# The entry of an output stage: order of the branch weights, buffers of the gates, staging of the last matrix

## The chip, the cores and the metric

The kernel runs on one core of a Trainium2 chip, in one launch. The metric is the device time of one execution in microseconds (us); the lower the better.

## What is computed

One layer of a streaming encoder, for 2048 prompt frames and 64 sample frames of 1024 channels. An input projection makes the parts of two branches (differential attention and retention), a gate path for each branch and two merge gates. The end of the layer is what matters here:

```python
def layer_output(x, oa, ob, za, zb, ga, gb, subln_g, lam_init, w_oa, w_ob, w_out):
    B, T = x.shape[0], x.shape[1]
    oa = (rmsnorm(oa, subln_g) * (1.0 - lam_init)).reshape(B, T, W_A) * jax.nn.silu(za)
    ob = rmsnorm(ob).reshape(B, T, W_B) * jax.nn.silu(zb)
    m = ga * (oa @ w_oa) + gb * (ob @ w_ob)
    return x + m @ w_out
```

`ga` and `gb` have gone through a sigmoid with a bias. `w_oa` and `w_ob` are 512 x 1024 (the branch weights `w_o_diff` and `w_o_ret`), `w_out` is 1024 x 1024.

## The kernel before

Every product keeps float32 accuracy by splitting each operand in a high part (a cast to a shorter float32, on ScalarE, ACT) and a remainder (a subtraction, on VectorE, DVE, or GpSimd, POOL), and by three matmuls: high x high, high x remainder, remainder x high.

The program is written out by a planner that runs while the kernel is built. Each piece of work is a generator with a priority (the second argument of `spawn`, small first). A generator yields a time or a condition; the planner keeps a model of the clock of each engine (`P`, `A`, `V`, `G`, `ld`) and always goes on with the first generator by priority that is ready on TensorE's (PE's) modelled clock. The order in which it emits instructions is the order on PE, ACT and DVE; on POOL and on SP's queue, from which all loads and stores are issued, the scheduler below it may issue an instruction earlier, once its buffer is free. `take` and `give` count the buffers of a tag; `BUFS` holds how many a tag has. Semaphores follow from the buffers.

Two streams share PE. `w_stream` does the input projections (L384) in two halves and ends the first part of the kernel; `z_stream` does attention and retention between them. When `z_stream` ends, its buffers are freed, the pool `z3` is opened there, and `load_wo` (priority 3) and `out_prep` (priority 1) are started, while PE is still in the last projections. `load_wo` brings each of the eight 128-row tiles of the branch weights in four pieces of 256 columns through `split_load` and `split_fin` (L1232, L1235, L1239), staged in buffers of the tag "oz". `out_prep` waits until the last weight tile has been set up, and then loads, for each group of 264 frames (256 prompt and 8 sample frames) and each of 8 tiles (4 per branch), a branch output `on` and its gate `z`; `og_fin` makes `on * silu(z)` with a third buffer `sg` and splits it (L1284 to L1301). These are the gated tiles, `ogh` and `ogl`.

When `w_stream` ends, its buffers are freed too and the pool `z4` is opened. `out_stream` (priority 8) then does PE's work of the output stage; `gate_prep` (priority 0) brings the merge gates, two buffers of the tag "gt" for each tile, and `load_wout` (priority 2) brings `w_out` in 32 pieces of 256 columns, staged in the same tag "gt", six buffers in all.

For each of 8 groups, `out_stream` runs 8 m tiles (L1339 to L1341), each 24 matmuls into one bank of the tag "mm" for branch A and one of the tag "s" for branch B, with two banks of each tag; `m_fin` multiplies them with the gates (L1359), adds (L1363), casts and subtracts (L1369 to L1377). Then two y tiles of 128 frames follow (L1404 to L1406), each 48 matmuls of 512 columns into two banks: rows 0 to 6 of `w_out` for the first half of the columns, rows 0 to 6 for the second, then row 7 for both. At the very end one more y tile, with 64 frames, does the sample frames that the groups have gathered in `ms`.

Of the kernel before, what the change touches and what calls it, by code (L numbers as in the profile page):

```python
# [8 lines left out]
F32 = mybir.dt.float32  # L9
F32R = mybir.dt.float32r  # L10
F16 = mybir.dt.float16
AF = mybir.ActivationFunctionType
# [14 lines left out]
GW = 264  # L27
# [8 lines left out]
        "oz": 9, "og": 17, "gt": 6, "m": 18, "xt": 2, "yt": 2}  # L36
# [18 lines left out]
class Hybrid:  # L55
# [1164 lines left out]
    def split_load(self, stp, tag, h, l, src, n, slot):  # L1220
        for q in range(4):
            sl = slice(256 * q, 256 * q + 256)
            yield from self.take(tag)
            s = self.sb(stp, [128, GW], tag, "wst")[:, :256]
            t = self.ld(s, src[:, sl], 1 << 17)
            self.spawn(self.split_fin(tag, h[:, sl], l[:, sl], s, t, (n + q) % 3 == 0, slot), 2)
            yield self.pe

    def split_fin(self, tag, h, l, s, t, on_pool, slot):
        nc = self.nc  # L1230
        yield t
        nc.scalar.copy(h, s)  # L1232
        t = self.A(256, self.pe)
        if on_pool:
            nc.gpsimd.tensor_sub(l, s, h.bitcast(F32))  # L1235
            t = self.G(256, t)
        else:
            yield t
            nc.vector.tensor_sub(l, s, h.bitcast(F32))  # L1239
            t = self.V(256, t)  # L1240
        self.give(tag, t)
        slot.append(t)

    def load_wo(self):
        pool = self.z3
        for br, name in enumerate(("w_o_diff", "w_o_ret")):
            for kt in range(4):
                h = pool.tile([128, 1024], F32R, tag=f"{name}h{kt}", name=f"{name}h{kt}")
                l = pool.tile([128, 1024], F32R, tag=f"{name}l{kt}", name=f"{name}l{kt}")
                slot = []  # L1250
                self.wo[br].append((h, l, slot))
                yield from self.split_load(pool, "oz", h, l, self.i[name][0, 128 * kt:128 * kt + 128, :], kt, slot)

    def load_wout(self):
        pool = self.z4
        for ct in range(8):
            h = pool.tile([128, 1024], F32R, tag=f"woh{ct}", name=f"woh{ct}")
            l = pool.tile([128, 1024], F32R, tag=f"wol{ct}", name=f"wol{ct}")
            slot = []
            self.wout.append((h, l, slot))  # L1260
            yield from self.split_load(pool, "gt", h, l, self.i["w_out"][0, 128 * ct:128 * ct + 128, :], ct, slot)

    def out_prep(self):
        pa = self.z3
        yield lambda: len(self.wo[1]) == 4
        for g in range(8):
            gsl = slice(GW * g, GW * g + GW)
            for br, (oT, zT) in enumerate(((self.oaT, self.zaT), (self.obT, self.zbT))):
                for kt in range(4):
                    yield from self.take("oz", 3)  # L1270
                    on = self.sb(pa, [128, GW], "oz", "on")
                    z = self.sb(pa, [128, GW], "oz", "z")
                    sg = self.sb(pa, [128, GW], "oz", "sg")
# [4 lines left out]
                    self.spawn(self.og_fin(on, z, sg, t, og), 1)  # L1278
                    yield self.pe

    def og_fin(self, on, z, sg, t, og):
# [10 lines left out]
        self.give("oz", t, 2)  # L1292
# [12 lines left out]

    def gate_prep(self):
        nc = self.nc
        pb = self.z4
        for g in range(8):
            gsl = slice(GW * g, GW * g + GW)  # L1310
            for ct in range(8):
                yield from self.take("gt", 2)
                pair = []
                for br, gT in enumerate((self.gaT, self.gbT)):
                    gt = self.sb(pb, [128, GW], "gt")
                    t = self.ld(gt, gT[ct][:, gsl], 1 << 17)
                    pair.append(gt)
                yield t
                for br in range(2):
                    nc.scalar.activation(pair[br], pair[br], AF.Sigmoid, bias=self.bg[:, br, ct:ct + 1])  # L1320
                    t = self.A(GW, t, 90)
                self.gts.append((pair, t))

    def m_tile(self, g, ct, og):
# [3 lines left out]
        for br, tag in ((0, "mm"), (1, "s")):  # L1328
            yield from self.take(tag)
            ps = self.psum(tag)[:, :GW]  # L1330
            for kt in range(4):
                wh, wl, tw = self.wo[br][kt]
                if ct == 0:
                    yield lambda: len(self.ogs) > 8 * g + 4 * br + kt and self.ogs[8 * g + 4 * br + kt] and len(tw) == 4
                    og.append(self.ogs[8 * g + 4 * br + kt][0])
                    if max(*tw, og[-1][2]) > self.pe:
                        yield max(*tw, og[-1][2])
# [12 lines left out]
    def m_fin(self, g, ct, pss):  # L1350
# [3 lines left out]
        gs, tg = self.gts.pop(0)  # L1354
# [24 lines left out]
        self.give("gt", t2, 2)  # L1379
        self.mq[g].append((h, l, t2))  # L1380

    def y_tile(self, g, sel, r, x, y):
# [10 lines left out]
        for ct, nh in [(c, k) for k in range(2) for c in range(7)] + [(7, 0), (7, 1)]:  # L1393
            nsl, xt, tx, ps = run[nh]
            yield lambda: len(self.wout) > ct and len(self.wout[ct][2]) == 4 and len(self.mq[g]) > ct
# [6 lines left out]
            if max(t, *tw) > self.pe:  # L1402
                yield max(t, *tw)
# [21 lines left out]
    def out_stream(self):  # L1425
        self.wout, self.gts = [], []
# [70 lines left out]
    def z_stream(self):  # L1497
# [28 lines left out]
        self.spawn(self.load_wo(), 3)  # L1526
        self.spawn(self.out_prep(), 1)

    def run(self):
# [14 lines left out]
        self.marks = {}  # L1544
        ET = mybir.EngineType
# [84 lines left out]
```

## Time and profile before

| | us |
|---|---|
| median of 3 runs | 2037.01 |
| lowest and highest run | 2036.58 and 2038.7 |
| the profiled execution's own time | 2037.63 |
| its span, first to last instruction | 2035.9 |
| first matmul of the output stage (from the span's start) | 1634.36 |

In the profile's rows PE is the matmul engine, PEld its weight loads, SPq the queue of SP. A row of the order of time gives start, duration, engine, line, operation and output<-input; in brackets stand the engine's idle time before it and what ended that. A row of the waits gives who waited for whom, the sum, how often, and the longest. A row of the windows gives the stretch, its length, then busy time and number of instructions of PE, PEld, DVE, ACT and POOL, the granted clock of PE, the share of the DMA engines and the GB/s moved. A row of a tile gives min/median/max of the duration in ns and the first and last start.

### The profile page before, as it was taken

Reading aid. Unit: us, or ns where it says so; the run is one execution under the profiler, and the core shown is the slowest. Engines: PE = TensorE matmul, PEld = TensorE weight load, DVE = VectorE, ACT = ScalarE, POOL = GpSimd, SP = SyncE. Lnnn points to the kernel's source line nnn. Section 1 sums busy time; section 2 is a strip of 40 time slices with the busy share of each in tenths; the row PEclk is TensorE's granted clock in tenths of the full one; section 3 lists DMA queues with packets and bytes.
Section 4 is the critical chain, followed back from the end, with each engine's and each line's share of the span. In section 5 each row is a group of like instructions: output and inputs, shape, how many; then the busy total and the mean of one; then the engine's idle time right before and its main releaser. Section 6 shows DMA issues by size and latency. Waiting matters only on the chain. (4 is left out here: it accounts for less than half of the span.)

```text
span 2035.9 us, 35819 instructions
## 1 busy us (share of the span) xinstructions
PE 1999.1 (98%) x13058; PEld 1826.1 (90%) x13058; DVE 985.9 (48%) x2671; ACT 962.7 (47%) x2123; POOL 420.5 (21%) x394
## 2 busy tenths in 40 slices
PE   7999999999999999999999999999999979999999
PEld 7999999999998999999999888888888868888997
DVE  6265765643331210546856545635653365444442
ACT  5334766644343332535766655634654453333321
POOL 1222112121012221221211212122131343222210
PEclk9999999999999999999999999999999989999999
DMA  6663545345565463563352252463233665454531
GB/s 217 202 195 115 162 138 145 101 124 156 151 170 133 130 194 93 152 200 127 113 155 91 84 154 75 115 188 99 63 100 113 187 200 154 144 150 136 148 101 58
DMA packets 332160, 281.57 MB, mean 138 GB/s; under 512 B 65104, under 2 KB 307408, under 8 KB 331984
## 3 DMA queue, kind: packets, MB, share of 16 engines
q1 hardware_dynamic: 331984, 279.29, 46.8%
q8 instruction: 103, 1.69, 0.4%
q14 instruction: 73, 0.60, 0.1%
HBM read 187.71 MB, written 91.49 MB: 137 GB/s over the span
## 5 line engine op out<-in xcount | busy, mean ns | idle before, releaser
L384 PE MATMUL mm<-xh,wh 128*128 128x512 f32 (+2 forms) x1280 | 459.8, 359 | 0.0
L384 PE MATMUL mm<-xh,wl 128*128 128x512 f32 (+2 forms) x1280 | 452.0, 353 | 0.0
L384 PE MATMUL mm<-xl,wh 128*128 128x512 f32 (+2 forms) x1280 | 451.7, 353 | 0.0
L361 POOL TENSOR_TENSOR wl<-ws,wh 128x512 fp32r<-128x512 f32 x190 | 252.1, 1342 | 832.5 <-ACT wh L354 643.5
L384 PE MATMUL mm<-wh,xh 128*128 128x256 f32 x1088 | 313.3, 288 | 0.5 <-ACT xh L315 0.3
L384 PE MATMUL mm<-wl,xh 128*128 128x256 f32 x1088 | 307.7, 283 | 0.7 <-DVE wl L358 0.3
L384 PE MATMUL mm<-wh,xl 128*128 128x256 f32 x1088 | 307.7, 283 | 0.2 <-DVE xl L316 0.2
L384 PEld LDWEIGHTS mm<-xh,wl 128*128 128x128 f32 x1280 | 241.0, 188 | 31.1
L384 PEld LDWEIGHTS mm<-xh,wh 128*128 128x128 f32 x1280 | 241.3, 189 | 30.6 <-issue 0.2
L384 PEld LDWEIGHTS mm<-xl,wh 128*128 128x128 f32 x1280 | 241.4, 189 | 30.0
L384 PEld LDWEIGHTS mm<-wh,xh 128*128 128x128 f32 x1088 | 204.8, 188 | 3.3 <-ACT xh L315 0.5
L384 PEld LDWEIGHTS mm<-wl,xh 128*128 128x128 f32 x1088 | 204.9, 188 | 3.0 <-DVE wl L358 0.5
L384 PEld LDWEIGHTS mm<-wh,xl 128*128 128x128 f32 x1088 | 204.7, 188 | 0.4 <-DVE xl L316 0.4
L569 ACT COPY ev<-mm 128x512 f32<-128x512 f32 x140 | 71.6, 512 | 213.4 <-PE mm L384 200.4
L865 DVE TENSOR_TENSOR atl<-at,ath 128x512 fp32r<-128x512 f32 (+1 forms) x144 | 93.6, 660 | 151.6 <-ACT ath L863 151.6
L782 ACT ACTIVATE row<-row,a_mx 128x1024 f32<-128x1024 f32 (+7 forms) x160 | 153.5, 963 | 24.2 <-DVE a_mx L762 24.0
L752 DVE CUSTOM_DVE_ANT_0 row<-s,dfar 128x512 f32<-128x512 f32 (+2 forms) x192 | 117.3, 631 | 72.4 <-PE s L744 71.3
L354 ACT CAST wh<-ws 128x512 fp32r<-128x512 f32 x192 | 117.0, 619 | 65.4 <-PE mm L384 37.5
L863 ACT CAST ath<-at 128x512 fp32r<-128x512 f32 (+1 forms) x144 | 79.6, 563 | 99.1 <-PE at L850 98.6
L743 PE MATMUL s<-K,q 128*128 128x512 f32 (+3 forms) x320 | 120.3, 381 | 3.0 <-DVE a_acc L752 2.8
L803 DVE SCALAR_TENSOR_TENSOR row<-row,a_w 128x1024 f32<-128x1024 f32 (+4 forms) x96 | 101.4, 1064 | 40.5 <-ACT row L800 40.2
L744 PE MATMUL s<-K,q 128*128 128x512 f32 (+3 forms) x320 | 115.7, 363 | 0.0
(196 smaller groups left out, 3922.1 us busy)
## 6 DMA issues: line engine op xcount, KB each, us to landing
ws<-in_w_in_dram SPq DMA_DIRECT2D x192, 256.0 KB, 3.0
q<-qT SPq DMA_DIRECT2D x128, 128.0 KB, 3.0
V<-vN SPq DMA_DIRECT2D x24, 512.0 KB, 5.4
K<-kT SPq DMA_DIRECT2D x48, 256.0 KB, 4.2
gt<-gaT SPq DMA_DIRECT2D x64, 132.0 KB, 2.1
gt<-gbT SPq DMA_DIRECT2D x64, 132.0 KB, 2.1
xt<-in_x_prompt_dram SPq DMA_DIRECT2D x16, 512.0 KB, 5.0
kn<-in_cache_k_T_dram SPq DMA_DIRECT2D x32, 256.0 KB, 3.2
```

The costliest lines, as they stand in the source:

```text
L354: nc.scalar.copy(h, st)
L361: nc.gpsimd.tensor_sub(l, st, h.bitcast(F32))
L384: nc.tensor.matmul(ps, p, q, start=c == 0 and i == 0, stop=c == KC - 1 and i == 2)
L569: nc.scalar.copy(ev, ps)
L743: nc.tensor.matmul(ps, q1s, kk, start=True, stop=False)
L744: nc.tensor.matmul(ps, q2s, kk, start=False, stop=True)
L752: nc.vector.tensor_tensor_reduce(out=units[k0 // 1024][:, k0 % 1024:k0 % 1024 + n], in0=ps, in1=tab, scale=-SLOPES[h], scalar=3.0e38, op0= ...
L782: nc.scalar.activation(u, u, AF.Exp, bias=mx, scale=-1.0, accum_out=lp[:, k:k + 1])
L803: nc.vector.scalar_tensor_tensor(out=u0, in0=u0, scalar=w[:, 0:1], in1=u1, op0=ALU.mult, op1=ALU.add)
L863: nc.scalar.copy(ah[:, :w], at[:, :w])
L865: nc.vector.tensor_sub(al[:, :w], at[:, :w], ah[:, :w].bitcast(F32))
```

## The change

- `out_prep` now sets up the branch weights itself, and loads them by column quarters, 8 loads for each quarter: quarter 0 first, then the eight gated tiles of group 0 and the gate pair of its first m tile (in two buffers of its own), then quarters 1 to 3, then groups 1 to 7. An m tile waits only for the quarter that it reads.
- A gated tile takes two buffers instead of three: POOL makes `on * z`, ACT makes the sigmoid of `z` in place, DVE multiplies both. "oz" has 8 buffers instead of 9, "og" 16 instead of 17.
- `w_out` is staged in a tag of its own, "wst", 4 buffers of 512 columns, in 16 loads: all first halves, then all second halves. A y tile waits only for the half that it reads. "gt" keeps its six buffers, now for gates alone.
- The last y tile does all rows of the first half, then all rows of the second.

```diff
-        "oz": 9, "og": 17, "gt": 6, "m": 18, "xt": 2, "yt": 2}
+        "oz": 8, "og": 16, "gt": 6, "wst": 4, "m": 18, "xt": 2, "yt": 2}
...
-    def split_load(self, stp, tag, h, l, src, n, slot):
...
-    def split_fin(self, tag, h, l, s, t, on_pool, slot):
+    def split_fin(self, tag, h, l, s, t, on_pool, slot, key):
...
-        slot.append(t)
+        slot[key] = t
...
-    def load_wo(self):
-        pool = self.z3
+    def load_wo(self, q):
+        sl = slice(256 * q, 256 * q + 256)
         for br, name in enumerate(("w_o_diff", "w_o_ret")):
             for kt in range(4):
...
-                yield from self.split_load(pool, "oz", h, l, self.i[name][0, 128 * kt:128 * kt + 128, :], kt, slot)
+                h, l, slot = self.wo[br][kt]
+                yield from self.take("oz")
+                s = self.sb(self.z3, [128, GW], "oz", "wst")[:, :256]
+                t = self.ld(s, self.i[name][0, 128 * kt:128 * kt + 128, sl], 1 << 17)
+                self.spawn(self.split_fin("oz", h[:, sl], l[:, sl], s, t, (kt + q) % 3 == 0, slot, q), 2)
+                yield self.pe
...
-            yield from self.split_load(pool, "gt", h, l, self.i["w_out"][0, 128 * ct:128 * ct + 128, :], ct, slot)
+        for nh in range(2):
+            sl = slice(512 * nh, 512 * nh + 512)
+            for ct in range(8):
+                h, l, slot = self.wout[ct]
+                yield from self.take("wst")
+                s = self.sb(pool, [128, 512], "wst")
+                t = self.ld(s, self.i["w_out"][0, 128 * ct:128 * ct + 128, sl], 1 << 18)
+                self.spawn(self.split_fin("wst", h[:, sl], l[:, sl], s, t, ct % 2 == 1, slot, nh), 2)
+                yield self.pe
...
     def out_prep(self):
         pa = self.z3
-        yield lambda: len(self.wo[1]) == 4
...
+        yield from self.load_wo(0)
         for g in range(8):
...
-                    yield from self.take("oz", 3)
+                    yield from self.take("oz", 2)
...
+            if g == 0:
+                pair = [pa.tile([128, GW], F32, tag=f"g0{br}", name="gt") for br in range(2)]
+                self.spawn(self.gate(0, 0, pair, None), 1)
+                for q in range(1, 4):
+                    yield from self.load_wo(q)
...
-        nc.scalar.activation(sg, z, AF.Sigmoid)
-        t = self.A(GW, self.pe)
-        yield t
-        nc.gpsimd.tensor_mul(z, z, sg)
-        t = self.G(GW, t)
+        nc.gpsimd.tensor_mul(on, on, z)
+        t = self.G(GW, self.pe)
+        yield t
+        nc.scalar.activation(z, z, AF.Sigmoid)
+        t = self.A(GW, t)
         yield t
         nc.vector.tensor_mul(on, on, z)
         t = self.V(GW, t)
-        self.give("oz", t, 2)
+        self.give("oz", t)
...
+    def gate(self, g, ct, pair, tag):
+        for br, gT in enumerate((self.gaT, self.gbT)):
+            t = self.ld(pair[br], gT[ct][:, GW * g:GW * g + GW], 1 << 17)
+        yield t
+        for br in range(2):
+            self.nc.scalar.activation(pair[br], pair[br], AF.Sigmoid, bias=self.bg[:, br, ct:ct + 1])
+            t = self.A(GW, t, 90)
+        self.gts.append((pair, t, tag))
+
     def gate_prep(self):
...
+        yield lambda: len(self.gts) > 0
+        for n in range(1, 64):
+            yield from self.take("gt", 2)
+            pair = [self.sb(self.z4, [128, GW], "gt") for _ in range(2)]
+            yield from self.gate(n // 8, n % 8, pair, "gt")
...
                 wh, wl, tw = self.wo[br][kt]
+                yield lambda: ct // 2 in tw
+                ready = tw[ct // 2]
...
-        for ct, nh in [(c, k) for k in range(2) for c in range(7)] + [(7, 0), (7, 1)]:
+        first = 8 if sel is None else 7
+        order = [(c, k) for k in range(2) for c in range(first)] + [(c, k) for c in range(first, 8) for k in range(2)]
+        for ct, nh in order:
             nsl, xt, tx, ps = run[nh]
-            yield lambda: len(self.wout) > ct and len(self.wout[ct][2]) == 4 and len(self.mq[g]) > ct
+            yield lambda: len(self.wout) > ct and nh in self.wout[ct][2] and len(self.mq[g]) > ct
...
-        self.spawn(self.load_wo(), 3)
         self.spawn(self.out_prep(), 1)
```

More of the change, by code (lines that the diff above doesn't have):

```diff
@@ L1378, in m_fin @@
         t2 = self.V(256, t1)
-        self.give("gt", t2, 2)
+        if gtag:
+            self.give(gtag, t2, 2)
         self.mq[g].append((h, l, t2))
@@ L1544, in run @@
         self.marks = {}
+        self.gts = []
         ET = mybir.EngineType
```

60 lines of the change are left out of this document (19 added, 41 removed).

## The prediction

> **What bounds the kernel now.** I read the page first, then the waits of PE over the output stage, then the windows, then PE's order of time at three places.
>
> ```profile
> span 2035.9 us, 35819 instructions
> ...
> PE 1999.1 (98%) x13058; PEld 1826.1 (90%) x13058; DVE 985.9 (48%) x2671; ACT 962.7 (47%) x2123; POOL 420.5 (21%) x394
> ```
>
> ```profile
> PE mm L1339 <- DVE gt L1359: 7.4, 4, 2.9
> PE s L1339 <- ACT ogh L1298: 4.6, 2, 4.3
> PE at L1404 <- ACT mh L1369: 2.0, 1, 2.0
> PE s L1340 <- DVE ogl L1301: 0.2, 1, 0.2
> ```
>
> ```profile
> 1590.00:1600.00 10.00, 10.00 (x46) 8.29 (x45) 3.01 (x6) 5.14 (x13) 4.15 (x6) 1.00 0.87 267
> ...
> 1640.00:1650.00 10.00, 7.29 (x39) 7.11 (x40) 6.21 (x13) 5.68 (x15) 4.55 (x6) 0.66 0.79 234
> ...
> 1800.00:2020.00 220.00, 219.48 (x1376) 198.77 (x1376) 98.36 (x268) 66.59 (x171) 49.27 (x64) 1.00 0.41 119
> ```
>
> PE is busy for 98% of the span, so the change can only win where PE rests. The second fence is every wait of PE from 1580 us to the end: 14.2 us, all in group 0 of the output stage. Before it (first window) and after it (last window, 219.48 of 220) PE has no rest. In the window between, the granted clock is 0.66, so the rests also slow the matmuls behind them. The whole loss is read from where a group's first matmul starts:
>
> ```profile
> 1634.36 0.28 PE L1339 MATMUL mm<-ogh,w_o_diffh 128*128 128x264 f32 x1
> 1634.48 0.28 PE L1340 MATMUL mm<-ogl,w_o_diffh 128*128 128x264 f32 x1
> ...
> 1643.78 0.42 PE L1339 MATMUL mm<-ogh,w_o_diffh 128*128 128x264 f32 x1
> 1644.00 0.42 PE L1340 MATMUL mm<-ogl,w_o_diffh 128*128 128x264 f32 x1
> ```
>
> ```profile
> 1700.75 0.28 PE L1339 MATMUL mm<-ogh,w_o_diffh 128*128 128x264 f32 x1
> ```
>
> ```profile
> 1746.36 0.28 PE L1339 MATMUL mm<-ogh,w_o_diffh 128*128 128x264 f32 x1
> ```
>
> Group 0 takes 1700.75 - 1634.36 = 66.4 us, group 1 takes 45.6. The entry therefore loses **20.8 us**: 14.2 of waits, and 6.6 because matmuls start 0.22 apart behind a rest (third fence, last two rows) where they start 0.12 apart otherwise. Nothing else in this kernel can be won by this change: 20.8 is its ceiling.
>
> **Part 1: the first gated tiles ahead of three quarters of the branch weights.** Today all 32 weight quarters are loaded and split before the first gated tile is loaded:
>
> ```profile
> 1589.45 4.86 SPq L130 DMA_DIRECT2D wst<-in_w_o_diff_dram  x9
> ...
> 1610.07 0.92 SPq L130 DMA_DIRECT2D wst<-in_w_o_ret_dram  x2
> 1611.08 0.38 SPq L130 DMA_DIRECT2D z<-zaT  x1
> ```
>
> ```profile
> 1641.44 0.92 ACT L1320 ACTIVATE gt<-gt,bg 128x264 f32<-128x264 f32 x2 [3.74 <-DMA gt<-gaT]
> 1642.27 0.39 ACT L1298 CAST ogh<-on 128x264 fp32r<-128x264 f32 x1
> ```
>
> ```profile
> L1239 DVE TENSOR_TENSOR w_o_retl<-wst,w_o_reth x10: 414/595/1547, 1604.6 to 1615.1; 128x256 fp32r<-128x256 f32 x10
> ```
>
> Weights go out in 21.5 us, 0.67 each. The eight gated tiles then take from 1611.1 to 1642.7, 31.6 us, with three in flight (nine buffers, three each); PE starts on them 8.3 us before the last is there. After: eight quarter-0 loads (out by 1594, at 0.54 each), then the tiles. Eight buffers at two each hold four in flight, so the tiles take between 31.6 x 3/4 = 23.7 and, if the buffer count isn't what paces them, 31.6 us: they end between 1618 and 1626, ahead of 1634.36. The other 24 quarters follow as buffers return: 24 x 0.67 = 16 us puts the last issue at 1634 to 1642, and 4 to 6 us later (today's last remainder starts at 1615.1, 4.1 after the last issue ends, and runs up to 1.5) the weights are whole, 1639 to 1647. Columns 768 and up are first read by the seventh m tile, at 1634.36 + 6 x 24 x 0.122 = 1651.9; quarter 1, by a third of that way, at about 1632 at the latest against 1640.2. So this costs PE nothing, with about 5 us of slack at the worst end, and the 4.6 + 0.2 of waits go. The cover is the projections' matmuls; without it each late microsecond would cost one.
>
> What is moved past what: on SP's queue the 24 loads go behind 16 tile loads and two gate loads, and the projections' last stores share that queue; a store held by a load that waits for a buffer holds an evacuation buffer, and with it a bank. I count nothing, since PE did not rest there beside the same loads in another order; the upper end is 2 us, the longest that an ACT step kept PE waiting apart from the gated tiles (third wait). On POOL the product now comes first, and the ACT sigmoid waits for it: queued behind it on ACT are the casts of weights and the evacuation copies, with two banks of slack. The number of instructions is the same, and the seventeenth gated buffer that goes was never used, since they are taken in twos.
>
> **Part 2: gates with buffers of their own.** Today the 32 loads of the output matrix share six buffers with the gate pairs:
>
> ```profile
> 1638.12 1.63 SPq L130 DMA_DIRECT2D gt<-gbT  x1
> 1639.80 1.85 SPq L130 DMA_DIRECT2D wst<-in_w_out_dram  x4
> ...
> 1643.80 0.33 SPq L130 DMA_DIRECT2D gt<-gaT  x1
> ...
> 1675.88 0.37 SPq L130 DMA_DIRECT2D gt<-gaT  x1
> ```
>
> ```profile
> 1705.16 0.33 SPq L130 DMA_DIRECT2D gt<-gaT  x1
> ...
> 1708.09 0.32 SPq L130 DMA_DIRECT2D gt<-gaT  x1
> ```
>
> A gate pair comes every (1675.88 - 1643.80)/5 = 6.4 us, against 2.9 us in the next group, which is the pace of an m tile (24 x 0.122). That gap is the 7.4 us on DVE's gating. After: pair 0 is ready long before; pairs 1 to 3 have free buffers at once. Costs of a pair's round:
>
> ```profile
> L1359 DVE TENSOR_TENSOR gt<-s,gt x64: 416/432/434, 1644.3 to 1998.3; 128x264 f32<-128x264 f32 x64
> L1363 POOL TENSOR_TENSOR gt<-gt x64: 738/755/937, 1645.2 to 1998.9; 128x264 f32<-128x264 f32 x64
> L1369 ACT CAST mh<-gt x64: 401/406/409, 1646.1 to 1999.7; 128x256 fp32r<-128x256 f32 x64
> ...
> DMA to landing us min/median/max: 1.9/2.1/3.6
> ```
>
> ```profile
> oxt<-in_x_prompt_dram SPq DMA_DIRECT2D x32, 256.0 KB, 3.5
> ```
>
> Pair 1 cannot come before today's first (its second load leaves at 1639.75): sigmoids done at 1642.4. Tile 3 needs the bank of tile 1 at 1643.1, so no rest. Pairs 2 and 3 go out behind four loads of 256 KB; with 3.6 us to landing and 0.92 of sigmoids they are ready at about 1646.5 and 1648, while PE has finished their tiles at 1643.1 and 1646.0: tile 4 waits for tile 2's product, about 1 us. From then on a buffer's round is two products, sum, cast, remainder (0.86 + 0.76 + 0.41 + 0.43, with handovers about 3.3), load 3.6 and sigmoids 0.92, 7.8 us against 3 x 2.92 = 8.8: it keeps up, with 1 us of slack. I take 1.5 us lost here; the ends are 0 and, with today's 6.4 us pace, 16 (rival B).
>
> **Part 3: the output matrix as 16 loads of 512 columns in four buffers.**
>
> ```profile
> L361 POOL TENSOR_TENSOR wl<-ws,wh 128x512 fp32r<-128x512 f32 x190 | 252.1, 1342 | 832.5 <-ACT wh L354 643.5
> ...
> L865 DVE TENSOR_TENSOR atl<-at,ath 128x512 fp32r<-128x512 f32 (+1 forms) x144 | 93.6, 660 | 151.6 <-ACT ath L863 151.6
> ...
> L354 ACT CAST wh<-ws 128x512 fp32r<-128x512 f32 x192 | 117.0, 619 | 65.4 <-PE mm L384 37.5
> ```
>
> These are the same shapes. One buffer's round is 3.5 to landing, 0.62, then 0.66 or 1.34: about 6.5 with handovers. Four rounds from 1639.8 end at about 1666. The first y tile starts at 1634.36 + 8 x 2.92 = 1657.7 plus what part 2 lost; it takes (45.6 - 23.4)/2 = 11.1 us, 0.69 for each row and half. It reads half 0 first (two rounds, 1653), and rows 4 to 7 of half 1 only 11 x 0.69 = 7.6 us in, at 1665 to 1669: the last round ends there too. I take 1.5 us of rest; 0 to 5. In bytes, 4.2 MB of matrix and 2 of gates by 1668 are 200 GB/s where 267 has been moved, so the transfers of group 1's tiles, which are not due before 1680, must give way a little.
>
> Against this stands a row, and a rule:
>
> ```profile
> L1290 DVE TENSOR_TENSOR on<-on,z x64: 419/426/993, 1621.5 to 1958.0; 128x264 f32<-128x264 f32 x64
> ```
>
> A DVE operation with both inputs in SBUF has been stretched from 0.43 to 0.99; the gating products, one input of which is a bank, never were (416/432/434). The change makes POOL's remainders 1.34 long. If a DVE remainder waits out one of these, a pair's round grows by up to 0.9 and its 1 us of slack is nearly gone; three rounds in a row matter, so 0.5 us of the residue below is for this. The Trainium skill, "SBUF — State Buffer", section "Who interferes with whom", has GpSimd and such DVE instructions lock each other out for a whole instruction; by it alone each of these could wait its full length, and the trace's 0.99 agrees.
>
> **Tail.** The last sample tile runs one half after the other. The second half's addition still follows the last matmul, so nothing is counted.
>
> **Sum.** From the profiled execution's 2037.63 (span 2035.9): minus 20.8, plus 1.5 + 1.5 + 0.5 = 3.5 of new rests, too short (each about 1 us) to bring the slow clock back: 2020.3. That execution stands 0.6 above the median 2037.01, so **2019.7**. With all rests at nothing 2015.6 to 2016.
>
> **Rivals.**
> A, the forecast: rests of 0 to 6 us, 2016 to 2022. For it: groups 1 to 7 run without a rest on six gate buffers. Chance 0.63.
> B, the pace of gates stays slow, since casts that wait for 256 KB loads stand ahead of sigmoids in ACT's fixed order. At 6.4 us, pair 5 is ready at 1642.4 + 25.6 = 1668.0, tile 7 ends at 1671.4, pair 7 is ready at 1680.8, its m tile 3.3 later, and the y tile ends 1.4 after, 1685.5 against 1657.7 + 11.1 = 1668.8 without rests: 17 us lost, 2033. At 5 us by the same steps 8.3 lost, 2024.6. Chance 0.17, middle 2028.
> C, the output matrix is late: rounds of 8 us instead of 6.5 end at 1672, 5 us more of rest, 2022 to 2026. Chance 0.10.
> D, slower: the sigmoid that now waits for POOL's product holds ACT in every group, and the casts and gate sigmoids behind it come late. A gate loaded at 1705.16 (its second half 0.9 later) is ready at 1709.1 and needed when its tile ends, at 1700.75 + 4 x 2.92 = 1712.4. So it decides only from 3.3 us of delay per tile; at 0.5 beyond that, 7 groups of 8 tiles lose 28, and the time is 2019.7 + 28 = 2048. Against it: a POOL operation of this size is 0.76 (L1363). Chance 0.06.
> E, nothing is moved: the entry rests elsewhere for the same 17 to 25 us (the weights' later quarters, say). It needs 20 us of lateness where part 1 has 5 in hand. Chance 0.04.
>
> **How the numbers follow.** Runs of this kernel differ by 2 us, so 0.2% (4.1 us) tells from no change. Faster: A, C and nearly all of B, 0.88; same: E and the end of B, 0.06; slower: D, 0.06. The range 2015.5 to 2028 holds A, C and half of B, 0.81.
>
> **What would show it.** Right: from 1634 on no wait of PE for ogh; the waits on the gating products under 2 us, no granted clock below 1.00 in the windows of the entry; first matmul of group 1 at 1683 to 1687; groups 1 to 7 still 45.6. Gate loads every 2.9 us from the fourth on. Wrong: PE resting inside the projections before 1634, waits of the y tiles on the output matrix's remainders of over 5 us, or gates still 6 us apart.

## The result, and the profile after

| | us |
|---|---|
| before, median of 6 runs | 2036.96 (2036.38 to 2038.70) |
| after, median of 6 runs | 2029.66 (2028.69 to 2033.04) |
| ratio, 95% interval | 0.9966, 0.9953 to 0.9979 |
| predicted | 2019.7 (2015.5 to 2028.0) |
| profiled execution of after, its span | 2033.04, 2031.1 |

The change makes the kernel faster, by 7.3 us. The prediction had 17.3, so its direction held and its size did not: the median lies 1.7 us above the top of its range. The profiled execution is the slowest of after's six runs, 3.4 us above their median, so its rests are likely some 3 us longer than those of a usual run. PE is busy for 98% of its span, as before; the entry has to be looked at by itself.

The waits of PE from 1580 us to the end, as before:

```profile
PE mm L1348 <- DVE gt L1368: 9.0, 3, 5.2
PE at L1418 <- DVE ml L1386: 2.5, 1, 2.5
PE at L1416 <- ACT mh L1378: 0.5, 1, 0.5
```

The wait for `ogh` is gone, as forecast. The wait on the gating products, which was to shrink to under 2 us, grew from 7.4 to 9.0. In PE's order of time the first matmuls of groups 0, 1 and 2 and the three rests on the gates are these:

```profile
1633.15 0.28 PE L1348 MATMUL mm<-ogh,w_o_diffh 128*128 128x264 f32 x1
...
1650.16 0.59 PE L1348 MATMUL mm<-ogh,w_o_diffh 128*128 128x264 f32 x1 [5.17 <-DVE gt L1368]
1656.98 0.39 PE L1348 MATMUL mm<-ogh,w_o_diffh 128*128 128x264 f32 x1 [1.70 <-DVE gt L1368]
1665.20 0.39 PE L1348 MATMUL mm<-ogh,w_o_diffh 128*128 128x264 f32 x1 [2.13 <-DVE gt L1368]
...
1696.62 0.28 PE L1348 MATMUL mm<-ogh,w_o_diffh 128*128 128x264 f32 x1
...
1742.09 0.28 PE L1348 MATMUL mm<-ogh,w_o_diffh 128*128 128x264 f32 x1
```

Group 0 takes 1696.62 - 1633.15 = 63.5 us where it took 66.4; group 1 takes 45.5, as before. In this execution the entry still loses 18.0 us: 12.0 of waits, and 6.0 that stand in no wait and come mostly from the slow clock behind the rests. The execution's time less group 0's length is 2033.04 - 63.5 = 1969.5, against 2037.63 - 66.4 = 1971.2 before. So of the 4.6 us between these two executions 2.9 lie in group 0. The other 1.7 cannot be put down to the change: over before, after and all the experiments below this difference spreads from 1969.4 to 1972.0, whatever the edit. By the same spread group 0 of a run at after's median takes an estimated 57.7 to 60.3 us, and its entry loses 12 to 15. The windows show what was busy there:

```profile
1644.00:1655.00 11.00, 5.83 (x33) 5.62 (x31) 8.92 (x14) 7.42 (x16) 7.12 (x6) 0.69 0.64 204
1655.00:1674.00 19.00, 14.38 (x95) 12.45 (x93) 18.19 (x36) 12.52 (x30) 12.18 (x12) 1.00 0.83 264
1674.00:1682.00 8.00, 5.77 (x14) 4.57 (x15) 6.64 (x11) 4.83 (x12) 5.09 (x6) 0.57 0.60 179
...
1650.00:1680.00 30.00, 22.99 (x125) 20.29 (x126) 29.04 (x53) 18.40 (x44) 20.81 (x19) 0.84 0.74 232
```

The same 30 us before:

```profile
1650.00:1680.00 30.00, 22.61 (x152) 21.04 (x150) 22.50 (x55) 19.46 (x53) 15.79 (x18) 0.94 0.66 201
```

The third busy figure is DVE's: it went from 22.50 to 29.04 of 30 us while it ran two instructions fewer. PE was busy hardly longer than before. The granted clock was low twice: about and behind the rest of 5.17 us (first window), and about and behind the 2.5 us for which a y tile waited for `ml` (third window). The rests of 1.70 and 2.13 us lie in the second window, where it stayed at 1.00.

How the longest rest came about is read from the order of time of SP's queue, ACT, POOL and DVE, in this order:

```profile
1638.79 1.85 SPq L130 DMA_DIRECT2D wst<-in_w_out_dram  x4
...
1641.91 0.43 SPq L130 DMA_DIRECT2D gt<-gaT  x1
...
1644.40 3.53 SPq L130 DMA_DIRECT2D wst<-in_w_out_dram  x3
1647.99 0.42 SPq L130 DMA_DIRECT2D gt<-gaT  x1
```

```profile
1645.07 1.94 ACT L1224 CAST woh<-wst 128x512 fp32r<-128x512 f32 x3 [1.88 <-DMA wst<-in_w_out_dram]
1646.92 0.40 ACT L1378 CAST mh<-gt 128x256 fp32r<-128x256 f32 x1
1647.49 0.92 ACT L1319 ACTIVATE gt<-gt,bg 128x264 f32<-128x264 f32 x2 [0.17 <-DMA gt<-gaT]
...
1652.26 0.92 ACT L1319 ACTIVATE gt<-gt,bg 128x264 f32<-128x264 f32 x2
```

```profile
1645.77 2.94 POOL L1227 TENSOR_TENSOR wol<-wst,woh 128x512 fp32r<-128x512 f32 x2 [2.28 <-ACT woh L1224]
```

```profile
1646.38 1.20 DVE L1231 TENSOR_TENSOR wol<-wst,woh 128x512 fp32r<-128x512 f32 x1 [2.01 <-ACT woh L1224]
1647.50 1.23 DVE L1381 CAST ms<-gt 128x8 fp32r<-128x8 f32 x1
1648.77 0.66 DVE L1382 TENSOR_TENSOR ms<-gt,ms 128x8 fp32r<-128x8 f32 x1
1649.35 0.41 DVE L1386 TENSOR_TENSOR ml<-gt,mh 128x256 fp32r<-128x256 f32 x1
1649.69 0.42 DVE L1368 TENSOR_TENSOR gt<-mm,gt 128x264 f32<-128x264 f32 x1
```

The third tile's gates are sent for at 1641.91, behind four loads of 256 KB, and land some 5 us later, where the prediction counted 3.6. Ahead of their sigmoids ACT has three casts of `w_out`, for whose landing it idled 1.88 us, and the cast of an `mh`. But it was done with them in time: it idled another 0.17 us until the pair itself had landed (the bracket of the third row), so for this pair the late sending and the landing counted, and not the casts. The gates are ready at 1648.4. DVE, which had itself stood 2.01 us for a cast of `w_out`, then still has to finish a cast of eight columns that takes 1.23 us beside two remainders on POOL, and two operations behind it. The product that frees PE's bank starts at 1649.69, and PE goes on at 1650.16. The next pair's load, 1647.99, stands in SP's queue behind three `w_out` loads that waited for staging buffers; its sigmoids start at 1652.26.

### The profile page after: what moved, and what is told of

Read it like the earlier page. It is cut to its first block, busy times and chain, and to the rows that moved or that the text cites. A ratio compares the mean times of both kernels' runs of the same rounds, so it can differ in the third digit from the quotient of the medians.

```text
span 2031.1 us, 35727 instructions
## 1 busy us (share of the span) xinstructions
PE 1997.0 (98%) x13058; PEld 1824.8 (90%) x13058; DVE 983.6 (48%) x2658; ACT 958.9 (47%) x2107; POOL 423.6 (21%) x391
## 4 chain that ended last, share of the span: by engine, by line
PE 93%; DVE 4%; DMA 1%; ACT 1%; issue 1%; SPq 0%; POOL 0%; DVEq 0%; ACTq 0%; POOLq 0%
PE mm L384 53%; PE s L743 3%; PE s L744 3%; PE at L1416 3%; PE at L1418 3%; PE at L1417 3%; PE at L850 3%; PE pv L830 2%; PE pv L829 2%; PE pv L828 2%; PE pv L1027 1%; PE s L1349 1%; PE s L1350 1%; PE mm L1350 1%; PE mm L1348 1%; PE s L1348 1%
```

## The experiments

The leading theory after this reading was rival B of the prediction: the gates stay slow, because their loads, sigmoids and products stand in fixed orders behind the staging of `w_out`. Against it stood three others: that DVE is the bound, stretched by POOL's long remainders (the lock theory); that the loads' volume delays the gates (the DMA theory); and that the wait for `ogh` had never been a loss of its own. Medians are compared with after's 2029.66; the median of before that was taken beside each experiment was between 2036.5 and 2037.3. PE's waits, in each fence, are those of the experiment's own profiled execution, from 1600 us on. A difference of 1 or 2 us between the waits of two single executions is not read.

### The parts by themselves

**order_only** is part 1 alone: the new order of branch weights and gated tiles and two-buffer gating, with `w_out` in 32 pieces in "gt" as before. **two_buf** is less still: two-buffer gating alone, with the weights ahead of the tiles as before. **staging_only** is "wst" and the halves, so the gates have their six buffers alone, with the entry's old order and three-buffer gating. The early first gate pair in two buffers of its own, which belongs to part 2, is in none of the three.

```diff
 order_only, against after
-        "oz": 8, "og": 16, "gt": 6, "wst": 4, "m": 18, "xt": 2, "yt": 2}
+        "oz": 8, "og": 16, "gt": 6, "m": 18, "xt": 2, "yt": 2}
...
-                yield from self.take("wst")
+                yield from self.take("gt")
...
-                pair = [pa.tile([128, GW], F32, tag=f"g0{br}", name="gt") for br in range(2)]
-                self.spawn(self.gate(0, 0, pair, None), 1)
...
 staging_only, against after
-        "oz": 8, "og": 16, "gt": 6, "wst": 4, "m": 18, "xt": 2, "yt": 2}
+        "oz": 9, "og": 17, "gt": 6, "wst": 4, "m": 18, "xt": 2, "yt": 2}
...
-        yield from self.load_wo(0)
+        yield lambda: len(self.wo[1]) == 4
...
 two_buf, against before
-        "oz": 9, "og": 17, "gt": 6, "m": 18, "xt": 2, "yt": 2}
+        "oz": 8, "og": 16, "gt": 6, "m": 18, "xt": 2, "yt": 2}
...
-                    yield from self.take("oz", 3)
+                    yield from self.take("oz", 2)
...
```

> Only the first part of the change: branch weights by column quarters around the first gated tiles and the two-buffer gating; the output matrix is staged in the six gate buffers in 32 pieces, and the first gate pair has no buffers of its own, as before. If the whole gain of the change came from the gated tiles being early (the 4.6 us wait and the slow clock behind it, together about 7) this alone gives 2030, as fast as the whole change. If the staging of its own gave a share, this stays between 2031 and 2035.

> Only the second part: the output matrix in 16 loads through four buffers of its own, gates alone in their six, the last tile half by half; weights and gated tiles in the old order with three buffers each. If the staging gave nothing net, 2036 to 2038. If it gave what the prediction counted for it (7.4 us of waits on the gating products and their slow clock), 2026 to 2029, with the 4.6 us wait for the gated tiles still there.

> The kernel before with the two-buffer gating alone (product on POOL first, sigmoid in place, four tiles in flight instead of three), all orders as before. The gated tiles of group 0 should all be there before 1638 instead of 1642.7. If the wait for them is a cost of its own, its 4.6 us and the slow clock go: 2030 to 2033. If the gates, which are ready at 1642.4, only take over the wait, as in the kernel with the new order alone (2040.5): 2036 to 2040.

| | median (range) | ratio to before | group 0 |
|---|---|---|---|
| order_only | 2040.55 (2038.82 to 2041.71) | 1.0018, 1.0009 to 1.0027 | 70.6 |
| two_buf | 2039.23 (2035.88 to 2040.77) | 1.0006, 0.9997 to 1.0015 | 68.2 |
| staging_only | 2032.66 (2030.89 to 2034.83) | 0.9982, 0.9973 to 0.9991 | 62.6 |

PE's waits in order_only, then in two_buf, then in staging_only:

```profile
PE mm L1345 <- DVE gt L1365: 14.0, 5, 3.7
PE at L1413 <- ACT mh L1375: 3.0, 1, 3.0
...
```

```profile
PE mm L1338 <- DVE gt L1358: 11.5, 5, 4.1
PE at L1403 <- ACT mh L1368: 1.7, 1, 1.7
...
```

```profile
PE s L1350 <- ACT ogh L1309: 4.4, 2, 4.1
PE mm L1350 <- DVE gt L1370: 3.5, 3, 2.1
PE at L1419 <- DVE ml L1388: 2.9, 2, 1.9
...
```

In the first two the wait for `ogh` is gone and the wait on the gating products is 14.0 and 11.5 instead of 7.4; neither is faster than before, and order_only is slower by 0.09% to 0.27%. While PE rested 4.6 us for `ogh`, the gates got on with theirs. Taken away alone, that rest comes back at the gates. Staging alone leaves it in place and halves the gates' wait. The parts do not add: 2040.55 and 2032.66 would, as separate gains, give 3.6 slower and 4.3 faster, 0.7 in all, where the whole change gives 7.3. How much of the missing 6.6 is their interplay, and how much the early first pair that neither has, was not measured.

### What the staging of w_out costs in after

**one_row** loads and splits only the first row of `w_out`. **loads_only** loads all of it but splits the first row alone. **splits_only** loads the first row alone but makes all casts and remainders. **casts_only** and **rems_only** load all and make only the casts, or only the remainders, of the other seven rows. All five leave a part of the last product out, or take it from the wrong row; they measure, and are no kernels to use.

```diff
 one_row
-            for ct in range(8):
+            for ct in range(1):
...
 loads_only
-                self.spawn(self.split_fin("wst", h[:, sl], l[:, sl], s, t, ct % 2 == 1, slot, nh), 2)
+                if ct == 0:
+                    self.spawn(self.split_fin("wst", h[:, sl], l[:, sl], s, t, ct % 2 == 1, slot, nh), 2)
+                else:
+                    self.give("wst", t + 2400)
...
 splits_only
-                s = self.sb(pool, [128, 512], "wst")
-                t = self.ld(s, self.i["w_out"][0, 128 * ct:128 * ct + 128, sl], 1 << 18)
+                if ct == 0:
+                    s = self.sb(pool, [128, 512], "wst")
+                    t = self.ld(s, self.i["w_out"][0, 128 * ct:128 * ct + 128, sl], 1 << 18)
...
 casts_only
-        if on_pool:
+        if not rem:
+            pass
+        elif on_pool:
...
 rems_only
-        nc.scalar.copy(h, s)
-        t = self.A(n, self.pe)
+        if cast:
+            nc.scalar.copy(h, s)
+            t = self.A(n, self.pe)
...
```

> The changed kernel with only the first of the eight row tiles of the output matrix loaded and split (2 loads instead of 16); all y tiles use it for every row, so that the output frames are left without seven eighths of the last product's weights. It shows what is left of the entry's loss when the staging is gone. If the staging is what makes the gates late (by its place in the queues, its volume or its remainders), the waits on the gating products fall under 2 us and the time to 2015 to 2019. If the gates' own round with six buffers is too slow, 2024 to 2029.

> The changed kernel with all 16 loads of the output matrix in their four buffers, but only the first row tile cast and split (2 of 16 pieces); the y tiles use it for every row, which leaves seven eighths of the last product's weights out. Between the kernel with one row tile loaded (2020) and the changed kernel (2029.7) it splits the staging's 9.7 us: theory of volume (the 4.2 MB make the gate loads late): 2026 to 2030; theory of the engines' work (casts on ACT, remainders on POOL and DVE, and their order): 2019 to 2023.

> The counterpart: the first row tile of the output matrix is loaded once for each half, and all 16 pieces are cast and split from it in the order and at the planned times of the changed kernel; seven eighths of the last product's weights are left out. Theory of the engines' work: 2026 to 2030, DVE busy over 27 of the 30 us from 1650 to 1680. Theory of volume: 2019 to 2023.

> The changed kernel with all 16 loads and all 16 casts of the output matrix, but remainders of the first row tile alone (its remainder serves every row, which is left out of the last product's accuracy). With loads alone 2021.9, with everything 2029.7. If casts on ACT, which wait for landings ahead of the sigmoids, are the cause: 2027 to 2030. If the remainders on DVE and POOL are: 2021.5 to 2024.

> The counterpart: all 16 loads and all 16 remainders, casts of the first row tile alone, against which all remainders are taken (the last product gets the wrong high parts for seven of eight rows). If the remainders are the cause: 2026 to 2030, with DVE's operations still stretched and DVE busy over 27 of the 30 us from 1650 to 1680. If the casts are: 2021.5 to 2024.

| | median (range) | ratio to before | above one_row |
|---|---|---|---|
| one_row | 2020.02 (2017.66 to 2021.94) | 0.9917, 0.9902 to 0.9931 | |
| loads_only | 2021.88 (2020.42 to 2023.85) | 0.9930, 0.9918 to 0.9943 | 1.9 |
| casts_only | 2027.64 (2026.55 to 2030.39) | 0.9959, 0.9947 to 0.9972 | 7.6 |
| splits_only | 2029.49 (2027.04 to 2032.12) | 0.9967, 0.9954 to 0.9979 | 9.5 |
| after | 2029.66 (2028.69 to 2033.04) | 0.9966, 0.9953 to 0.9979 | 9.6 |
| rems_only | 2032.19 (2029.19 to 2034.11) | 0.9979, 0.9970 to 0.9988 | 12.2 |

For one_row, loads_only, splits_only, casts_only and rems_only in turn, first the row of PE's waits on the gating products, then the window from 1650 to 1680:

```profile
PE mm L1349 <- DVE gt L1369: 2.3, 1, 2.3
```

```profile
1650.00:1680.00 30.00, 29.77 (x165) 25.61 (x165) 18.75 (x45) 13.92 (x37) 11.18 (x14) 1.00 0.62 183
```

```profile
PE mm L1352 <- DVE gt L1372: 4.4, 3, 2.7
```

```profile
1650.00:1680.00 30.00, 28.25 (x159) 24.48 (x158) 17.84 (x45) 15.62 (x39) 10.74 (x14) 0.98 0.87 270
```

```profile
PE mm L1352 <- DVE gt L1372: 7.1, 3, 3.9
```

```profile
1650.00:1680.00 30.00, 23.73 (x127) 20.59 (x128) 27.07 (x52) 17.15 (x42) 21.21 (x19) 0.85 0.44 129
```

```profile
PE mm L1351 <- DVE gt L1371: 9.1, 3, 3.2
```

```profile
1650.00:1680.00 30.00, 24.02 (x126) 22.09 (x126) 16.69 (x44) 18.13 (x45) 9.12 (x12) 0.83 0.68 217
```

```profile
PE mm L1350 <- DVE gt L1370: 12.4, 3, 6.3
```

```profile
1650.00:1680.00 30.00, 21.90 (x117) 20.65 (x118) 22.71 (x50) 12.51 (x32) 16.95 (x18) 0.75 0.74 228
```

With nearly all of the staging gone the kernel takes 2020.0, close to the 2019.7 forecast for the whole. Its group 0 takes 48.6 us, 3.0 more than its group 1, where 3.5 of rests were forecast. So the rest of the change does what it was to do, and the staging costs 9.6 us. The DMA theory falls as the main cause: with all loads and 270 GB/s only 1.9 us come back, within the spread of the runs; with all splits and 129 GB/s the whole loss is back. It is the casts and remainders, not the bytes.

Which of the two is not to be said. Casts alone bring back 7.6 us with DVE busy for only 16.69 of 30 us, so a full DVE is not needed for the loss, and the lock theory cannot be the whole. Remainders alone cost at least as much as both together (12.2 against 9.6, with ranges that overlap). Each version has another order on ACT, DVE and POOL, since the planner writes it anew, and in each the same product comes late by another way. In casts_only ACT stood for `w_out` to land, with the sigmoids behind, as in after (6.3 us there); in rems_only and in splits_only ACT stood for POOL's gate sums. The three rows below, of ACT's waits from 1636 to 1690 in casts_only, rems_only and splits_only, show it. In splits_only ACT has no wait for `w_out` at all in this stretch, and the whole loss is there: that casts wait for a landing is thus not needed for it.

```profile
ACT woh L1224 <- DMA wst<-in_w_out_dram: 6.5, 4, 2.9
```

```profile
ACT mh L1380 <- POOL gt L1374: 10.5, 6, 4.1
```

```profile
ACT mh L1382 <- POOL gt L1376: 11.0, 4, 4.0
```

### One remedy at a time, and together

**gates_ahead** makes a generator of each gate pair, so that a load need not wait for the landing of the pair before. **rem_dve** puts all remainders of `w_out` on DVE, at 0.66 us each instead of POOL's 1.34. **rem_halves** leaves them on POOL and cuts each in two of 256 columns. **late_casts** makes the planner hold each cast of `w_out` 3 us longer, so that ACT need not stand for a landing with sigmoids behind. **ahead_dve** is gates_ahead and rem_dve together.

```diff
 gates_ahead
-            yield from self.gate(n // 8, n % 8, pair, "gt")
+            self.spawn(self.gate(n // 8, n % 8, pair, "gt"), 0)
+            yield self.pe
 rem_dve
-                self.spawn(self.split_fin("wst", h[:, sl], l[:, sl], s, t, ct % 2 == 1, slot, nh), 2)
+                self.spawn(self.split_fin("wst", h[:, sl], l[:, sl], s, t, False, slot, nh), 2)
 rem_halves
-            nc.gpsimd.tensor_sub(l, s, h.bitcast(F32))
-            t = self.G(n, t)
+            for k in range(0, n, 256):
+                c = slice(k, k + 256)
+                nc.gpsimd.tensor_sub(l[:, c], s[:, c], h[:, c].bitcast(F32))
+                t = self.G(256, t)
 late_casts
-                self.spawn(self.split_fin("wst", h[:, sl], l[:, sl], s, t, ct % 2 == 1, slot, nh), 2)
+                self.spawn(self.split_fin("wst", h[:, sl], l[:, sl], s, t + 3000, ct % 2 == 1, slot, nh), 2)
```

> The changed kernel, with the gate pairs loaded as soon as two buffers are free, without first waiting for the pair before to land and be put through the sigmoid. Pairs 1 to 3 then leave ahead of the output matrix's first loads, and their sigmoids stand ahead of its casts. Theory of order (gate loads and sigmoids stand in the queues behind loads and casts of the output matrix): the waits on the gating products fall from 9.0 to under 3 us, time 2018 to 2023. Theory of the lock (DVE is held by POOL's 1.34 us remainders): the first wait (5.2) shrinks by 2 to 3 us and the others stay, 2026 to 2028. Theory of volume (the transfers as such are late): no change, 2029 to 2031.

> The changed kernel, with all 16 remainders of the output matrix on DVE (0.68 us each) and none on POOL, which had 8 at 1.34. Theory of the lock: DVE's operations are no longer stretched (1.2 to 1.8 us where 0.16 to 0.68 is their length), DVE's busy time in the entry falls although it does 8 more, and the time falls by 3 to 8 us, 2022 to 2027. Theory of order: DVE has 5.4 us more to do in its fixed order ahead of the gating products, 2029 to 2033.

> The changed kernel, with each remainder that POOL makes of the output matrix in two instructions of 256 columns (about 0.74 each) instead of one of 512 (1.34); same loads, same casts. Theory of the lock: a DVE operation waits for the end of one POOL instruction, so at most 0.74 instead of 1.34; DVE's busy time from 1650 to 1680 falls from 29.1 to 26 to 27.5, time 2026 to 2029. Theories of order and volume: DVE's busy time and the time stay, 2029 to 2031.

> The changed kernel, with the cast of each piece of the output matrix put 3 us later in the written order (the plan supposes that much more time to landing). Theory of order: ACT no longer waits for a landing with sigmoids and casts of the gates behind it, waits on the gating products 9.0 to 5 or less, time 2024 to 2027. Theory of the lock: the remainders on POOL are still there, and the matrix comes later, so 2028 to 2033.

> Both edits that gained: gate pairs loaded ahead, and all remainders of the output matrix on DVE. If order and lock are two causes, the gains (2.4 and 2.3 us) add: 2023 to 2026, waits on the gating products under 2. If they are one wait seen from two sides: 2026 to 2028.

| | median (range) | ratio to before | against after |
|---|---|---|---|
| gates_ahead | 2027.23 (2026.09 to 2028.50) | 0.9957, 0.9944 to 0.9969 | -2.4 |
| rem_dve | 2027.37 (2026.54 to 2031.79) | 0.9962, 0.9949 to 0.9974 | -2.3 |
| rem_halves | 2028.90 (2027.55 to 2032.53) | 0.9958, 0.9944 to 0.9972 | -0.8 |
| late_casts | 2031.60 (2030.67 to 2034.74) | 0.9975, 0.9966 to 0.9985 | +1.9 |
| ahead_dve | 2026.27 (2024.70 to 2027.09) | 0.9947, 0.9932 to 0.9962 | -3.4 |

The waits of gates_ahead, the window of rem_dve, and the waits of late_casts:

```profile
PE mm L1349 <- DVE gt L1369: 3.8, 2, 2.6
PE at L1417 <- ACT woh L1224: 2.2, 1, 2.2
...
```

```profile
1650.00:1680.00 30.00, 24.36 (x129) 21.05 (x130) 25.34 (x59) 19.84 (x47) 13.36 (x14) 0.84 0.81 249
```

```profile
PE mm L1348 <- DVE gt L1368: 5.6, 3, 3.7
PE at L1416 <- ACT woh L1224: 3.0, 1, 3.0
PE at L1418 <- DVE ml L1386: 2.3, 1, 2.3
```

Earlier gate loads take the gating wait from 9.0 to 3.8 us, and the high parts of `w_out` become late in their place. Of the four single remedies this is the only one whose runs all lie below after's.

rem_dve gives DVE six instructions more than after has, and DVE is busy 3.7 us less in this stretch: POOL's remainders had stretched it by more than the work that it took over. That much of the lock theory is shown. What it is worth in time is not: the medians differ by 2.3 us, but the ranges of rem_dve and after overlap, and the intervals of their ratios overlap nearly whole. rem_halves cannot be told from after either.

late_casts, the simplest reading of rival B, is no gain. It does what it was to do, since ACT has no wait for `w_out` from 1636 to 1690, where after had 6.3 us. The gates' wait falls to 5.6 and the y tiles wait 5.3 instead of 3.0, so the rest moved from the gates to the y tiles. Together the two remedies give 3.4, less than their 4.7 apart, though by less than the runs spread.

### A better version

**pre8** adds to ahead_dve a quarter of `w_out`, eight pieces of 256 columns, loaded behind the branch weights through "oz", whose buffers are free before the output stage starts. **pre8_low** also gives group 1's gated tiles a lower priority, and **pre8_half** also holds the second halves of `w_out` until the sixth m tile.

```diff
 pre8, against ahead_dve
...
+                for k in range(8):
+                    yield from self.take("oz")
+                    w = self.sb(pa, [128, GW], "oz", "wpre")[:, :256]
+                    self.pre.append((w, self.ld(w, self.i["w_out"][0, 128 * (k // 2):128 * (k // 2) + 128,
+                                                                   256 * (k % 2):256 * (k % 2) + 256], 1 << 17)))
+                    yield self.pe
...
 pre8_low, against pre8
-                    self.spawn(self.og_fin(on, z, t, og), 1)
+                    self.spawn(self.og_fin(on, z, t, og), 1 if g == 0 else 3)
 pre8_half, against pre8_low
+            yield lambda: nh == 0 or self.mt >= 5
...
```

> The fastest so far (gate pairs ahead, remainders on DVE: 2026.3) with the first quarter of the output matrix (rows 0 to 511 of half 0, 8 loads of 256 columns) put into the eight buffers of the gated tiles right behind the last branch weights, before the projections end, so that 1 MB less is to be loaded in the entry; the tiles of group 1 are loaded behind it. Theory of volume: 2022 to 2025. Theory of the engines' work: the casts and remainders are the same, and group 1's tiles fall into the entry: 2025 to 2029.

> The kernel with the first quarter of the output matrix loaded ahead (2024.5), with the steps that finish the gated tiles of groups 1 to 7 put behind the pieces of the output matrix in the plan's priority. If DVE's load in the entry is what is left, its order matters: 2021 to 2024. If not, 2024 to 2027, or slower where group 1 then starts late.

> As the kernel before in this list, and the second half of the output matrix is loaded only once five m tiles of group 0 have been written out, so that its eight remainders stand behind the gating products of the first tiles. If DVE's load is what is left: waits on the gating products under 2 us, 2020 to 2023; if the second half then comes late for the first y tile: 2025 to 2030 with waits of the y tiles on the remainders.

pre8 takes 2024.54 (2023.38 to 2026.06; 0.9942, 0.9930 to 0.9954), pre8_low 2023.84 (0.9942, 0.9929 to 0.9956), pre8_half 2024.18 (0.9943, 0.9930 to 0.9955). They are one result: 12 to 13 us below before and some 5 below after, the fastest that computes everything. pre8_low and pre8_half say nothing of their two suspects, since they hardly reached the entry: about the rest ACT and DVE have nearly the same order in all three, and the first load of a second half leaves at 1649.48 us in pre8, at 1650.32 in pre8_low and at 1651.22 in pre8_half. Of PE's waits two are left, here those of pre8, with ACT's sigmoids and DVE's operations ahead of the first:

```profile
PE mm L1363 <- DVE gt L1383: 3.5, 1, 3.5
PE at L1433 <- DVE ml L1401: 2.3, 1, 2.3
```

```profile
1649.24 0.92 ACT L1333 ACTIVATE gt<-gt,bg 128x264 f32<-128x264 f32 x2 [0.23 <-DVE wol L1231]
```

```profile
1650.04 0.68 DVE L1231 TENSOR_TENSOR wol<-wst,woh 128x512 fp32r<-128x512 f32 x1
...
1651.97 1.28 DVE L1231 TENSOR_TENSOR wol<-wst,woh 128x512 fp32r<-128x512 f32 x2
...
1653.51 0.42 DVE L1383 TENSOR_TENSOR gt<-mm,gt 128x264 f32<-128x264 f32 x1
```

The gates are ready at 1650.16 and their product starts at 1653.51. In between DVE is busy without a break, with the last three remainders of the first halves and three steps of earlier m tiles, and with no tile of group 1. So in pre8 this rest hangs on what stands ahead of the product in DVE's order.

## Why the prediction was right and wrong, step by step

**The ceiling of 20.8 us, and the place.** Right as far as the runs go: no experiment goes below it, and one_row, without seven eighths of the staging, comes to 17 of the 20.8. Its own sum with all rests at nothing gives 2016.2 (2019.7 less 3.5), where the prediction has 2015.6 to 2016.

**Part 1, the gated tiles in time, no cost on PE.** Right as told: the tiles were whole at 1618.7 (forecast 1618 to 1626) and the weights at 1637.9 (forecast 1639 to 1647), with no wait for `ogh`, none for a branch weight, none in the projections. Wrong as a term of the sum: the 4.6 + 0.2 were counted as won, when the gates' readiness lay right behind them. The prediction itself had the row that says so, the pace of a gate pair, 6.4 us against 2.9. By two_buf the term was worth nothing before the gates were mended.

**Part 2, free buffers for pairs 1 to 3, 1.5 us lost.** This is the step that failed: 9.0 us were lost in the profiled execution. Four of its terms were short. The pair for tile 2 was to be ready at 1646.5 and was at 1648.4, the next at 1648 and was at 1653.2 (its sigmoids start at 1652.26 and take 0.92). A free buffer does not send for a load: by the planner's clock `gate_prep` asks for a pair only when the one before has landed, as the diff shows, and `w_out` loads that wait for staging stand between, as SP's rows show. The prediction took the buffers alone. From pair 4 on the loads left at 1653.79, 1657.47, 1663.29 and 1666.07, 4.1 us apart, where 2.9 was forecast. And the round of 7.8 us counted bare durations, without a queue on ACT or DVE: tile 2's product started 1.3 us after its gates were ready.

In sum, new rests were to cost 3.5 us, and the entry lost 18.0 in that execution (an estimated 12 to 15 at the median): the gates 7.5 more than forecast, the y tiles 1.5 more, and 6.0, mostly slow clock, for which nothing was counted, less the 0.5 kept for the lock. What the runs show in place of free buffers is that `w_out`'s casts and remainders hold the gates, 9.6 us by one_row.

**Part 3, 1.5 us on the output matrix.** The y tiles rested 3.0 us, but on `ml` and `mh`, late with the gates; `w_out` itself kept PE waiting nowhere in after. It did once the gates were faster (2.2 us in gates_ahead).

**The lock term, 0.5 us.** The mechanism was right, the size too small for DVE's time (3.7 us in 30, by rem_dve); in the kernel's time it may be some 2 us, which the noise does not settle. The prediction asked only what a stretched remainder does to a pair's round. It left out that DVE as a whole would be full. The Trainium skill, "SBUF — State Buffer", section "Who interferes with whom", has a VectorE operation with two SBUF inputs contend with a GpSimd operation that reads SBUF, and says that a cast can contend too, one of the two then fully blocked for the whole instruction of the other. The trace agrees, since the eight-column cast that starts at 1647.50 ends at 1648.73, when the two POOL remainders end (1645.77 + 2.94 = 1648.71).

**Rests too short for the slow clock.** Not refuted, since the longest rests were not short. The slow clock came about the 5.17 us and the 2.5 us, and the 6.0 us that are mostly its work are nearly the 6.6 of before. The two rests of 1.70 and 2.13 us left the granted clock at 1.00. So this term failed with part 2.

**The rivals.** B came nearest: its span was 2024.6 to 2033 and its middle 2028, and pairs 1 to 7 were sent for 4.7 us apart on the mean (1637.90 to 1666.07), close to the quicker of its two paces. It got 0.17, since the six buffers that suffice in groups 1 to 7 were taken for proof; there no `w_out` stands between. The cut of the range at 2028 left out B's upper half, where the time fell. Its cause, casts that wait for landings ahead of sigmoids, held at most in part: late_casts and splits_only have no such wait and the loss all the same. D did not come: group 1 still takes 45.5. Of the three signs that were to show the prediction wrong, a rest before 1634 and 5 us on `w_out`'s remainders did not come, and gates 6 us apart only for pairs 3 and 4 (6.1 and 5.8). It was told by signs of being right that stayed away: waits on the gates under 2 us, and group 1 from 1683 to 1687, which began at 1696.62.

**What stays open.** How the 9.6 us divide between ACT's order, DVE's fill and SP's order. Every cut also rewrote the orders, and the cuts do not add up. More buffers for the gates or for `w_out` were not tried.

## What to carry to other kernels

A wait that ends last can cover the next one, so before it is counted as won, the time at which the next input is ready has to be worked out; removing the covering wait alone can even cost. Buffers are only one of the things that send a load off: the generator that asks, the queue that it stands in and the engine orders behind landings each have to be followed for the first rounds, where a stage starts cold. To find which part of a staging hurts, keep its loads and drop its work, and the reverse: here that took two runs and left the bytes at most some 2 us of 9.6.

## What the runs showed of the hardware

- A VectorE cast of 128 x 8, 0.16 us undisturbed, took 1.23 us beside GpSimd remainders of 128 x 512; a remainder of 128 x 256 took up to 1.51 us instead of 0.41, one of 128 x 512 up to 1.77 instead of 0.68. With GpSimd's remainders moved to it, VectorE was less busy, 25.34 us instead of 29.04 of 30.
- The transfers went faster than before or after asked in the same stretch (201 and 232 GB/s): loads_only moved 270 GB/s over 30 us and took 1.9 us longer than one_row, which moved 183.
- The length of a rest alone did not decide whether PE's clock fell. In after it stayed at 1.00 about rests of 1.70 and 2.13 us. A rest of 2.73 us was followed by a granted clock of 0.50 in loads_only (1648 to 1650), and one as long in before, which ended at 1673.03, by 1.00.
